# Output stores alternate between the SyncE and the GpSimd queue

## The chip, the cores and the metric

The kernel runs on one core of a Trainium2 chip. The metric is the device time of one execution in microseconds (us), the median of several runs. The profile is one further execution on the same kind of chip, recorded by the hardware profiler. Its span (first to last instruction) is a little shorter than the device time.

## The reference

A mixture-of-experts dispatch reduced to its arithmetic: each of 16 x 1024 tokens has a row of 512 floats and k = 2 weights. The output holds the row twice, each copy times one of the weights. The expert indices are an input that nothing reads.

```python
batch, seq, hidden, k = 16, 1024, 512, 2
x_expanded = x[:, :, np.newaxis, :].repeat(k, axis=2)
weights = expert_weights[..., np.newaxis]
return (x_expanded * weights).astype(np.float32)
```

So 33.6 MB of float32 are read, 67.1 MB are written, and each output element costs one multiplication.

## The kernel before, in words

The 16,384 tokens are cut into 8 groups of 2,048. In a group, each of the 128 partitions holds 16 consecutive tokens (16 "columns" of 512 floats), so that a partition's share of a load is one contiguous 32 KB row in memory. A group's load is one transfer of 4.19 MB (4,096 KB) into one of two `x_tile` buffers (`x_pool`, `bufs=2`). The group's output is two tiles of 8 columns, each 4.19 MB as well: a column holds both copies of a token. They come from a pool of four `o_tile` buffers (`o_pool`, `bufs=4`). A group thus moves three transfers of equal size: a load and two stores.

Weights: eight small loads (16 KB each, L55), one for each group, are issued on SyncE's queue at the start, ahead of all stores.

Compute: for every column, ScalarE multiplies the row by the second weight (`nc.scalar.mul`, L91) and VectorE by the first (`nc.vector.tensor_scalar`, L97). Each engine therefore runs 8 instructions for an output tile and 16 for a group, 128 in all. When both have done the eight columns of a tile, it is stored by one transfer (L105) on SyncE's queue. That store's landing is what frees the output buffer for the tile four later.

Loads: those of groups 0 and 1 are issued at the start, on ScalarE's queue (L76). The load of group i+2 takes the buffer that group i has read, so it waits for both engines' last multiply of group i. In the built program it stands on ScalarE just behind the first multiply of group i+1. That multiply in turn waits for the load of group i+1 and for a free output buffer, so the next load is issued when group i+1 starts.

The order of the work is that of the program: the framework puts a wait where a tile is read, written or reused, and gives each transfer one of a set of completion semaphores, in turn. SyncE has nothing to do but issue the weight loads and the stores. GpSimd sets four constants at the start and does nothing else. The end of the program (L134) waits for all transfers.

The lines around the change:

Of the kernel before, what the change touches and what calls it, by code (L numbers as in the profile page):

```python
# [1 line left out]

# [4 lines left out]


@with_exitstack
def kernel(  # L10
    ctx: ExitStack,
    tc: tile.TileContext,
    x: bass.AP,
    expert_indices: bass.AP,
    expert_weights: bass.AP,
    out: bass.AP,
):
    nc = tc.nc

    batch, seq, hidden = x.shape  # L20
    k = expert_weights.shape[-1]
    P = nc.NUM_PARTITIONS
    ntok = batch * seq
    assert ntok % P == 0
    A_TOTAL = ntok // P

    f32 = mybir.dt.float32
    row = k * hidden
    TX = 16
    TO = 8  # L30


    groups = [[16], [16], [16], [16], [16], [16], [16], [16]]
    assert sum(sum(g) for g in groups) == A_TOTAL

    xf = x.rearrange("b s h -> (b s) h")
    of = out.rearrange("b s k h -> (b s) (k h)")
    wf = expert_weights.rearrange("b s k -> (b s) k")

    w_pool = ctx.enter_context(tc.tile_pool(name="w_pool", bufs=1))  # L40
    x_pool = ctx.enter_context(tc.tile_pool(name="x_pool", bufs=2))
    o_pool = ctx.enter_context(tc.tile_pool(name="o_pool", bufs=4))

    w_tile = w_pool.tile([P, A_TOTAL * k], f32)

    def rows(of_all, done, T):
        return of_all[done * P : (done + T) * P, :].rearrange(
            "(p a) n -> p (a n)", a=T
        )

    weights = []
    for group in groups:
        weights.append((sum(n for _, n in weights), sum(group)))
    for at, T in weights:
        nc.sync.dma_start(out=w_tile[:, at * k : (at + T) * k], in_=rows(wf, at, T))  # L55

    tiles = []
    done = 0
    for group in groups:
        T = sum(group)  # L60
        a0 = 0
        for n in group:
            tiles.append((done, T, a0, n))
            a0 += n
        done += T

    loaded = []

    def load(i):
        if i >= len(tiles):  # L70
            return
        done, T, a0, n = tiles[i]
        x_tile = x_pool.tile([P, TX * hidden], f32)
        cols = rows(xf, done, T)[:, a0 * hidden : (a0 + n) * hidden]
        for lo, hi in [(0, P)]:
            nc.scalar.dma_start(out=x_tile[lo:hi, : n * hidden], in_=cols[lo:hi, :])  # L76
        loaded.append(x_tile)

    for i in range(2):
        load(i)  # L80
    for i, (done, T, a0, n) in enumerate(tiles):
        x_tile = loaded[i]
        outr = rows(of, done, T)
        for t in range(n):
            if t % TO == 0:
                o_tile = o_pool.tile([P, TO * row], f32)
            for kk in range(k):
                c = (done + a0 + t) * k + kk
                o = t % TO * row + kk * hidden
                if kk == 1:  # L90
                    nc.scalar.mul(  # L91
                        out=o_tile[:, o : o + hidden],
                        in_=x_tile[:, t * hidden : (t + 1) * hidden],
                        mul=w_tile[:, c : c + 1],
                    )
                    continue
                nc.vector.tensor_scalar(  # L97
                    out=o_tile[:, o : o + hidden],
                    in0=x_tile[:, t * hidden : (t + 1) * hidden],
                    scalar1=w_tile[:, c : c + 1],  # L100
                    scalar2=None,
                    op0=mybir.AluOpType.mult,
                )
            if (t + 1) % TO == 0:
                nc.sync.dma_start(  # L105
                    out=outr[:, (a0 + t + 1 - TO) * row : (a0 + t + 1) * row],
                    in_=o_tile,
                )
        load(i + 2)

# [1 line left out]
_INS = ['x', 'expert_indices', 'expert_weights']  # L112
_OUTS = [((16, 1024, 2, 512), 'float32')]


# [23 lines left out]
```

## Time and profile before

| What | Value |
|---|---|
| Time, median of 3 runs | 240.27 us (240.18 to 241.31) |
| Span of the profiled execution | 238.4 us |
| VectorE busy | 51.9 us (22%), 128 multiplies of 480 ns |
| ScalarE busy | 81.3 us (34%), 128 multiplies of 708 ns |
| HBM read, written | 33.69 MB, 67.11 MB: 423 GB/s over the span |
| A load, issue to landing | 23.2 us (median) |
| A store, issue to landing | 48.3 us (median) |

How to read the profile: ACT is ScalarE, DVE VectorE, POOL GpSimd, SP SyncE; ACTq and SPq are their instruction queues, which issue transfers. An issue is not the transfer: the issuing instruction takes some 0.33 us, while the 16 DMA engines move the data later. The rows of digits cut the span into 40 slices of about 6 us; a 9 is a slice busy for 90% or more. In the list of queues, q1 is SyncE's and q10 is ScalarE's, each with packets, MB and its packets' time as a share of 16 engines' span. In the waits, a row has the waiting engine and line, what it waited for, the sum in us, how often, and the longest. In the timeline, a row has start, length and instruction; in brackets is the idle time ahead of it with what ended it. Where a group of the timeline has several multiplies of one engine, "mean" durations include overlap of neighbours, so 8 of ScalarE's take 5.01 us and not 8 x 708 ns.

### The profile page before, as it was taken

The numbers are of one execution on the slowest core, as the hardware profiler recorded it, in microseconds if no ns is written. First come the engines' busy times: TensorE is split into PE (matmuls) and PEld (weight loads), VectorE is DVE, ScalarE is ACT, GpSimd is POOL, SyncE is SP. The second block draws the span as 40 slices with busy tenths as digits, with TensorE's granted clock in tenths as the row PEclk, the third lists the DMA queues.
The fourth block names the chain that finished last, engine by engine and source line by source line (L and its number), as shares of the span: only waits on it lengthen the run. The fifth ranks groups of instructions, "written<-read, shape, count | busy, mean of one in ns | idle before, by whom it ended". The sixth has DMA issues, their size and how long they took to land.

```text
span 238.4 us, 384 instructions
## 1 busy us (share of the span) xinstructions
DVE 51.9 (22%) x128; ACT 81.3 (34%) x129; POOL 0.2 (0%) x4
## 2 busy tenths in 40 slices
DVE  0072910055005004050230503204040235000000
ACT  0278970086207007080260803417043256200000
POOL 0000000000000000000000000000000000000000
DMA  7999999999999999999999999999999999999996
GB/s 266 441 442 357 441 429 412 423 429 429 440 440 440 437 434 434 440 440 418 423 429 423 434 440 440 434 440 434 440 429 440 434 429 412 429 429 440 440 440 264
DMA packets 4610, 100.81 MB, mean 423 GB/s; under 512 B 1536, under 2 KB 1536, under 8 KB 1536
## 3 DMA queue, kind: packets, MB, share of 16 engines
q1 hardware_dynamic: 3456, 67.24, 65.6%
q10 hardware_dynamic: 1152, 33.55, 33.2%
q14 instruction: 2, 0.02, 0.0%
HBM read 33.69 MB, written 67.11 MB: 423 GB/s over the span
## 4 chain that ended last, share of the span: by engine, by line
DMA 60%; another core or an unknown queue 12%; ACT 12%; ACTq 1%; issue 0%
DMA out_dram<-o_tile 41%; DMA x_tile<-in_x_dram 16%; ACT o_tile L91 12%; DMA w_tile<-in_expert_weights_dram 3%; ACTq L76 0%; ACTq L134 0%; ACTq L91 0%
## 5 line engine op out<-in xcount | busy, mean ns | idle before, releaser
L91 ACT ACTIVATE o_tile<-x_tile,w_tile 128x512 f32<-128x512 f32 x128 | 80.1, 708 | 113.9 <-DMA out_dram<-o_tile 96.1
L97 DVE TENSOR_SCALAR o_tile<-x_tile,w_tile 128x512 f32<-128x512 f32 x128 | 51.9, 480 | 150.4 <-DMA out_dram<-o_tile 115.6
L91 ACT ACT_TABLE_LOAD x1 | 1.3, 1283 | 8.7 <-DMA w_tile<-in_expert_weights_dram 8.7
L123 POOL MEMSET const-bfloat16-1.0<- 128x1 bf16 x1 | 0.1, 101 | 0.0
L123 POOL MEMSET const-uint8-127<- 128x1 uint8 x1 | 0.1, 101 | 0.0
L123 POOL MEMSET const-float32-0.0<- 128x1 f32 x1 | 0.1, 98 | 0.2 <-issue 0.2
L123 POOL MEMSET const-float32-1.0<- 128x1 f32 x1 | 0.1, 98 | 0.0
## 6 DMA issues: line engine op xcount, KB each, us to landing
out_dram<-o_tile SPq DMA_DIRECT2D x16, 4096.0 KB, 48.3
x_tile<-in_x_dram ACTq DMA_DIRECT2D x8, 4096.0 KB, 23.2
w_tile<-in_expert_weights_dram SPq DMA_DIRECT2D x8, 16.0 KB, 21.1
```

Of the source, the lines that this page charges most:

```text
L91: nc.scalar.mul(out=o_tile[:, o : o + hidden], in_=x_tile[:, t * hidden : (t + 1) * hidden], mul=w_tile[:, c : c + 1],)
L97: nc.vector.tensor_scalar(out=o_tile[:, o : o + hidden], in0=x_tile[:, t * hidden : (t + 1) * hidden], scalar1=w_tile[:, c : c + 1], scala ...
L123: nc = _bacc.Bacc("TRN2", target_bir_lowering=False, num_devices=1)
```

## The change

The store of a group's first output tile stays on SyncE's queue, that of its second goes to GpSimd's. Each then issues eight of the sixteen stores. Loads stay on ScalarE's queue and the weights on SyncE's. The purpose is to have the stores on two queues, so that one store need not stand behind the one before it in the same queue.

```diff
             if (t + 1) % TO == 0:
-                nc.sync.dma_start(
+
+                store = nc.sync if t // TO % 2 == 0 else nc.gpsimd
+                store.dma_start(
                     out=outr[:, (a0 + t + 1 - TO) * row : (a0 + t + 1) * row],
                     in_=o_tile,
                 )
```

`TO` is 8, and `t` runs over the group's 16 columns, so `t // TO % 2` is 0 for the first tile and 1 for the second. In the changed kernel the store's line is L107, and the end of the program is L136.

## The prediction

> **What bounds the kernel now.** I read the page's DMA rows first, since two compute engines at 22% and 34% can't be the bound.
>
> ```profile
> DVE 51.9 (22%) x128; ACT 81.3 (34%) x129; POOL 0.2 (0%) x4
> DMA  7999999999999999999999999999999999999996
> GB/s 266 441 442 357 441 429 412 423 429 429 440 440 440 437 434 434 440 440 418 423 429 423 434 440 440 434 440 434 440 429 440 434 429 412 429 429 440 440 440 264
> ...
> q1 hardware_dynamic: 3456, 67.24, 65.6%
> q10 hardware_dynamic: 1152, 33.55, 33.2%
> ```
>
> The 16 DMA engines are at 9 in every slice but the first and the last. Queue q1 (SyncE's: 16 stores of 4.19 MB and the weights) and q10 (ScalarE's: 8 loads) took 65.6 + 33.2 = 98.8% of 16 engines' span. That is 235.5 of 238.4 us, so 2.9 us are idle: by the packet records about 1.9 us before the first packet and 0.9 us after the last. Nothing is idle between. A tile of 4.19 MB at 432 GB/s is 9.7 us of all the engines; 24 of them are 233 us.
>
> Next, the waits, and the issues.
>
> ```profile
> DVE o_tile L97 <- DMA out_dram<-o_tile: 115.6, 11, 13.8
> ACT o_tile L91 <- DMA out_dram<-o_tile: 96.1, 11, 12.0
> DVE o_tile L97 <- DMA x_tile<-in_x_dram: 34.7, 3, 17.1
> ACT o_tile L91 <- DMA x_tile<-in_x_dram: 17.7, 3, 13.6
> ```
>
> ```profile
> out_dram<-o_tile SPq DMA_DIRECT2D x16, 4096.0 KB, 48.3
> x_tile<-in_x_dram ACTq DMA_DIRECT2D x8, 4096.0 KB, 23.2
> ```
>
> The compute engines wait 11 times for a store to free one of the four output buffers, and only 3 times (the first groups) for a load: output buffers hold the kernel back, and always with stores queued, 48.3 us from issue to landing, five times a tile's 9.7. A load lands 23.2 us after its issue. If one load and one store share the engines evenly it needs 2 x 9.7 = 19.4 us; the other 3.8 us pass before its first packet (the packet records say 3.9 for the load issued at 72.97). Last, the timeline, one group of 16 columns:
>
> ```profile
> 102.30 0.72 ACT L91 ACTIVATE o_tile<-x_tile,w_tile 128x512 f32<-128x512 f32 x1 [8.38 <-DMA out_dram<-o_tile]
> 102.34 3.26 DVE L97 TENSOR_SCALAR o_tile<-x_tile,w_tile 128x512 f32<-128x512 f32 x8 [10.07 <-DMA out_dram<-o_tile]
> 102.38 0.33 ACTq L76 DMA_DIRECT2D x_tile<-in_x_dram  x1
> 102.93 4.38 ACT L91 ACTIVATE o_tile<-x_tile,w_tile 128x512 f32<-128x512 f32 x7
> ...
> 131.30 0.72 ACT L91 ACTIVATE o_tile<-x_tile,w_tile 128x512 f32<-128x512 f32 x1 [8.38 <-DMA out_dram<-o_tile]
> ...
> 198.93 5.01 ACT L91 ACTIVATE o_tile<-x_tile,w_tile 128x512 f32<-128x512 f32 x8 [4.62 <-DMA out_dram<-o_tile]
> ```
>
> A group's first multiply and its load issue stand together (102.30 and 102.38), a group takes 29.0 us (131.30 - 102.30), and it moves three tiles: 3 x 9.7 = 29.1. So a load issued at a group's start lands 5.8 us (29.0 - 23.2) before the next group could use it. The last multiply ends at 203.9, 34 us before the end: stores alone fill the tail.
>
> **What the Trainium skill says.** *DMA: Bandwidth & Descriptors*, section "Issuing engines are not separate DMA queues": transfers from any engine interleave on the same 16 engines, and several issuers save only issue time. The trace agrees that there is little to save: 0.33 us per issue, hidden. Same page, "Queues, rings and completion order": each DMA engine takes the queues that have work in turn, a packet at a time. The 23.2 us above fit an even split of two. Same page, "SWDGE vs HWDGE vs iDMA": a GpSimd transfer has its descriptors written by GpSimd's cores into rings in SBUF. No run here shows it yet. *SBUF — State Buffer*, "Who interferes with whom": a two-port VectorE instruction, which a tensor_scalar can be, blocks GpSimd from the shared port, and so such a store's start. In before GpSimd issues nothing.
>
> **The change part by part.** Bytes, buffers and multiplies stay. In the built instruction order the other engines' sequences are unchanged, ScalarE still waits for a store tile by tile, and the waits on reused DMA semaphores still point to transfers long landed. Four things change.
>
> *Issue.* Eight of 16 stores leave SyncE's queue: 8 x 0.33 us less there, worth nothing, as SyncE sits waiting for the multiplies.
>
> *Descriptors.* GpSimd writes them for 8 stores. The skill's first byte is about 1 us against 0.6 (its page's "Specifications"); it is hidden wherever a few us of other transfers are queued, as they are by the reckoning below. VectorE's lock hardly matters: a store waits for ScalarE's 8 x 0.63 = 5.0 us, while VectorE's 8 take 3.26 us, and both tiles of a group (6.42 us in the opening groups) are done before ScalarE's 10. I take 0; upper end one burst, 3.3 us, once.
>
> *Row size.* Rows go as packets of 32 KB at 1,213 ns, and 128 B ones take 13 ns (packet records): about 8 ns fixed each. If software cuts rows to 4 KB, a row has 7 more, 56 ns; 1,024 rows over 16 engines make 3.6 us, at 2 KB 7.7 us. "The descriptor swizzle" (same page) has 8 KB rows whole in a 1 MiB transfer, so I take uncut: 0.
>
> *Shares.* This is the step that can move the end. With stores pending on two queues, a load gets a third and not half: 3 x 9.7 + 3.8 = 33 us from issue to landing, where the group has 29. The 5.8 us of slack are gone, so loads become the gate and stores drain in between. I reckoned this by hand from the first store at 23.6 us: a load gets 1/2 beside one busy store queue and 1/3 beside two; the next load's first packet comes 4.1 us after a landing (less when little is queued); a group's stores are issued 5.1 and 10.1 us after its start. Loads 2 to 7 (from 0) then land at about 57, 91, 124, 154, 181 and 212 us, and the store work still queued is 14.6, 10.5, 6.4, 5.7, 7.0 and 5.6 us. The queue never empties between loads: it shrinks until one store queue runs dry for a while, and the load gets its half again. So the middle costs 0. In the tail, group 7 starts at 212 and not at 189 as in before. Its first store goes out 5.1 us later and needs 1.3 us to its first packet (first issue 0.7 us, first packet 2.0). The 5.6 us of queue cover 6.4 us but for 0.8; then two tiles follow. With 0.3 for a GpSimd start that is not fully hidden the sum is +1.1 us: 240.27 + 1.1 = 241.4. The queue at the last landing is the soft number: sharing or start times a little different make it 3 to 7, so the hole is 0 to 3.4 us.
>
> **Rivals.**
> (a) *Hidden anyway.* The queue at the last landing is 6.4 us or more, as in two of the last four landings reckoned above (6.4 and 7.0). Nothing shows: 240.3. For it: transfers are saturated and bytes equal. Against: the last reckoned queue is 5.6.
> (b) *Software rows cost.* Cut at 4 KB: 240.27 + 3.6 + about 1 = 245; at 2 KB 249. For it: no such transfer in the trace. Against: 8 KB rows are whole in the skill.
> (c) *Loads starved.* If GpSimd's ring gets more than its turn (a packet of several rows), the store queue is empty at the last landing, 6.4 us idle: 247; with 1.6 us lost at each of six landings more, 256.
> (d) *Faster.* Some packets in the opening took about 2 us and not 1.2; the slice at 18 to 24 us moved 357 GB/s, not 441. Packets over 1,213 ns add 1.5 us per engine in all. If other interleaving removes them and the tail has no hole: 238.8. Against: they come at the first load and at the first store, which stay where they are. There are no other idle microseconds to win.
>
> **How the numbers follow.** Forecast (small hole in the tail) 0.45, (a) 0.30, (b) 0.11, (c) 0.08, (d) 0.06. The bound for "slower" is 241.47; over half of the forecast's spread (240.8 to 243.7) lies above it. Slower: 0.27 + 0.11 + 0.08, near 0.47; same 0.30 + 0.17 = 0.47; faster 0.06. The range goes from 239.9, leaving most of (d) out, to 246.5, which takes in the whole hole and rows cut at 4 KB, and leaves out 2 KB rows and starved loads.
>
> **What would show it.** Right: ScalarE's and VectorE's waits move from the stores to the loads (up to 8 waits each, one for each group); the median load from issue to landing rises from 23.2 to 27 to 33 us; the last multiply ends near 222 and not 203.9; DMA slices stay 9 up to the last tenth, and a dip of 1 to 3 us stands about 217. Wrong in the shares: loads still land in about 23 us and the stores remain the wait. Wrong in the row size: the GpSimd queue has more than 1,024 data packets plus increments, or a larger sum of the queues' shares x span than 235.5 us. Wrong as in (c): dips at every group.

## The result and the profile after

The changed kernel takes 253.18 us (median; 250.68 to 254.11), the kernel before 240.23 us: a ratio of 1.051 (95% interval 1.043 to 1.060). It is slower by 5%, far beyond the forecast of 241.4 us and above the range. Each profile is of one execution. The ratios here and below leave out single runs that lie more than 1.5% above the fastest of the same kernel.

The page of the changed kernel, its DMA rows and its queues (q0 is GpSimd's):

```profile
span 251.0 us, 388 instructions
...
DMA  7999999999999999999998999999999999996995
GB/s 290 435 435 355 423 407 355 397 345 418 392 402 433 402 428 428 431 402 428 418 433 355 386 428 428 428 418 350 428 465 428 433 418 423 454 392 272 433 418 251
...
q10 hardware_dynamic: 1152, 33.55, 33.2%
q1 hardware_dynamic: 2304, 33.69, 33.0%
q0 software_dynamic: 1152, 33.55, 31.0%
```

The digits hardly differ from those of before: the DMA engines still count as busy nearly everywhere. The GB/s row is what gives the change away: slices of 345 to 407 GB/s under a 9. The same bytes take longer. By the shares, packets took 98.8% of 238.4 = 235.5 us per DMA engine before and 97.2% of 251.0 = 244.0 us now. GpSimd's queue has 1,152 packets: 1,024 rows of 32 KB and 128 increments of semaphores, so its rows are not cut.

The waits, and the issues with their median time to landing:

```profile
DVE o_tile L97 <- DMA x_tile<-in_x_dram: 178.8, 8, 31.9
ACT o_tile L91 <- DMA x_tile<-in_x_dram: 144.3, 8, 28.4
```

```profile
x_tile<-in_x_dram ACTq DMA_DIRECT2D x8, 4096.0 KB, 30.3
out_dram<-o_tile SPq DMA_DIRECT2D x8, 4096.0 KB, 31.3
out_dram<-o_tile POOLq DMA_DIRECT2D x8, 4096.0 KB, 33.7
```

All waits for stores have gone; every group now waits for its load. And the timeline of the last group:

```profile
223.78 9.91 ACT L91 ACTIVATE o_tile<-x_tile,w_tile 128x512 f32<-128x512 f32 x16 [20.34 <-DMA x_tile<-in_x_dram]
```

It starts at 223.8 us, where the last one of before ended at 203.9.

**Where 12.6 us of span came from.** The packet records add up, per DMA engine (mean of 16): packets longer by 8.5 us (244.1 against 235.6, increments and weights included); idle between first and last packet 3.5 us against none; 0.6 us more from the last packet to the end of the span. The sum is 12.6. In both kernels the median packet of 32 KB takes 1,213 ns. After the first 26 us, 2 of 2,777 such packets were over that by more than 0.1 us before, and 288 of 2,775 in the changed kernel, these with a mean of 1.67 us. Of the 288, 274 are on the two hardware queues: what packets took beyond 1,213 ns after the opening sums, per DMA engine, to 4.2 us on SyncE's queue, 4.0 on ScalarE's, and 0.2 on GpSimd's own.

The long packets are not spread over the whole run. All but one of the 288 start before 174 us. From 174 to 230 us none of 700 is long, though all three queues have packets there (256 on GpSimd's, 272 on SyncE's, 172 on ScalarE's).

**The DMA engines fall out of step.** Each of these transfers raised its semaphore 16 times, once for each DMA engine, and landed with the last. The trace keeps all 16 times (us, sorted; it does not name the engines):

```text
before, a load    182.3 182.4 182.5 182.5 182.5 182.5 182.6 182.6 182.9 183.0 183.0 183.2 183.5 183.6 183.7 183.8
changed, a store   86.2  86.4  86.5  86.6  86.6  86.7  86.8  87.0  87.1  87.3  90.2  90.4  90.7  92.5  93.0  94.2
changed, load 7   212.6 212.6 212.7 212.7 212.7 212.7 212.7 212.8 214.2 214.3 216.1 217.8 217.9 218.0 223.7 223.7
```

Load 7 is that of the last group. Before, first and last are never more than 2.2 us apart; in the changed kernel up to 16.3. For the last group's load, ten DMA engines were done by 214.3, two needed until 223.7, and the group, which starts at 223.8, waited for those two.

### The profile page after: what moved, and what is told of

The parts are those of the page before. It is cut to its first block, busy times and chain, and to the rows that moved or that the text cites. A ratio compares the mean times of both kernels' runs of the same rounds, so it can differ in the third digit from the quotient of the medians.

```text
span 251.0 us, 388 instructions
## 1 busy us (share of the span) xinstructions
DVE 51.4 (20%) x128; ACT 80.7 (32%) x129; POOL 4.6 (2%) x12
## 3 DMA queue, kind: packets, MB, share of 16 engines
q10 hardware_dynamic: 1152, 33.55, 33.2%
q0 software_dynamic: 1152, 33.55, 31.0%
## 4 chain that ended last, share of the span: by engine, by line
DMA 88%; DVE 2%; issue 2%; POOLq 0%; ACT 0%; DVEq 0%; ACTq 0%
DMA x_tile<-in_x_dram 85%; DMA w_tile<-in_expert_weights_dram 3%; DVE o_tile L97 2%; POOLq L136 0%; ACT o_tile L91 0%; DVEq L136 0%; ACTq L91 0%; DVEq L97 0%; POOLq L107 0%
## 5 line engine op out<-in xcount | busy, mean ns | idle before, releaser
L91 ACT ACTIVATE o_tile<-x_tile,w_tile 128x512 f32<-128x512 f32 x128 | 79.4, 708 | 144.4 <-DMA x_tile<-in_x_dram 144.3
L97 DVE TENSOR_SCALAR o_tile<-x_tile,w_tile 128x512 f32<-128x512 f32 x128 | 51.4, 480 | 178.8 <-DMA x_tile<-in_x_dram 178.8
L107 POOL DMA_DIRECT2D out_dram<-o_tile x8 | 4.4, 550 | 229.7 <-ACT o_tile L91 229.7
## 6 DMA issues: line engine op xcount, KB each, us to landing
x_tile<-in_x_dram ACTq DMA_DIRECT2D x8, 4096.0 KB, 30.3
out_dram<-o_tile SPq DMA_DIRECT2D x8, 4096.0 KB, 31.3
out_dram<-o_tile POOLq DMA_DIRECT2D x8, 4096.0 KB, 33.7
```

Of the source, the lines that this page charges most:

```text
L91: nc.scalar.mul(out=o_tile[:, o : o + hidden], in_=x_tile[:, t * hidden : (t + 1) * hidden], mul=w_tile[:, c : c + 1],)
L97: nc.vector.tensor_scalar(out=o_tile[:, o : o + hidden], in0=x_tile[:, t * hidden : (t + 1) * hidden], scalar1=w_tile[:, c : c + 1], scala ...
L107: store.dma_start(out=outr[:, (a0 + t + 1 - TO) * row : (a0 + t + 1) * row], in_=o_tile,)
```

## The experiments

Three theories. A: the third busy queue (two of stores and one of loads) is at fault, through the load's share or through the rotation itself. B: a GpSimd queue harms its neighbours. C: two queues that write neighbouring 32 KB rows harm each other. Diffs are against the changed kernel.

| Run | Busy queues | Time, us (range) | Ratio to before, 95% | Packets, us too long | Landings apart, median / max |
|---|---|---|---|---|---|
| before | 2 | 240.2 | 1 | 1.6 | 0.9 / 2.2 |
| changed | 3 | 253.2 | 1.043 to 1.060 | 10.0 | 6.0 / 16.3 |
| all stores on GpSimd | 2 | 242.0 | 1.003 to 1.008 | 2.1 | 1.3 / 3.1 |
| stores on ScalarE and SyncE | 2 | 242.8 | 1.006 to 1.016 | 3.3 | 0.9 / 4.3 |
| alternating by group | 3 | 249.6 | 1.028 to 1.041 | 5.3 | 4.8 / 18.8 |
| second tile's rows far away | 3 | 254.8 | 1.049 to 1.061 | 10.9 | 4.9 / 16.7 |
| three x, three output buffers | 3 | 250.1 | 1.033 to 1.042 | 4.1 | 3.7 / 13.8 |
| the same, one store queue | 2 | 240.8 | 1.000 to 1.003 | 1.5 | 1.4 / 2.5 |
| 16 KB store rows | 3 | 243.3 | 1.007 to 1.014 | 1.8 | 2.3 / 5.8 |
| the same, one store queue | 2 | 247.3 | 1.017 to 1.030 | 3.9 | 4.6 / 12.0 |

"Too long" sums, per DMA engine, what packets took beyond 1,213 ns (611 ns for 16 KB), the opening included. "Apart" is between a transfer's first and last engine, in us, over all loads and stores. The packet and landing columns are of one execution each.

**1. All stores on GpSimd**

```diff
-                store = nc.sync if t // TO % 2 == 0 else nc.gpsimd
+                store = nc.gpsimd
```

> All sixteen stores on GpSimd, loads on ScalarE: two busy queues, one of them software. Theory A (a third busy queue takes the load's share and lengthens packets): about 240 us, loads land in about 23 us and the waits are for stores, packets beyond 1,213 ns add under 2 us per DMA engine. Theory B (a GpSimd queue by itself lengthens the packets of the other queues): 248 us or more, long packets among ScalarE's loads.

241.99 us (241.63 to 242.75). The waits are those of before:

```profile
DVE o_tile L97 <- DMA out_dram<-o_tile: 105.8, 10, 15.0
ACT o_tile L91 <- DMA out_dram<-o_tile: 96.5, 11, 13.2
```

Packets are 2.1 us too long in all, against 1.6. Theory B falls as it was put: GpSimd as the only store queue costs 0.55%, not 5%.

**2. Loads on GpSimd, stores on ScalarE and SyncE**

```diff
-            nc.scalar.dma_start(out=x_tile[lo:hi, : n * hidden], in_=cols[lo:hi, :])
+            nc.gpsimd.dma_start(out=x_tile[lo:hi, : n * hidden], in_=cols[lo:hi, :])
-                store = nc.sync if t // TO % 2 == 0 else nc.gpsimd
+                store = nc.scalar if t // TO % 2 == 0 else nc.sync
```

> Three queues with the roles changed: loads on GpSimd, stores alternate between ScalarE (first tile) and SyncE (second). Theory A: as in the changed kernel, 248 to 255 us, loads land in about 30 us or more, waits for loads, a hole of about 4 us before the last group's stores. Theory B with GpSimd's part in the transfers equal (8 of 24): long packets on the hardware queues as well, same time. Theory C (two store queues that write neighbouring 32 KB rows are what lengthens packets): also slow. This run says only whether GpSimd must carry stores.

Four times: 244.01, 281.61, 285.9 and 286.31 us. None is in theory A's 248 to 255, and no ratio and no cause is drawn from so wide a scatter. The profile is of the 286.31 and tells of that execution alone: landings of one transfer up to 41 us apart, and whole slices in which most DMA engines are idle while a few finish:

```profile
DMA  7999999999999999999899994698972996039940
```

Packets too long come to 9.8 us per DMA engine and idle time to 37.7. So DMA engines can fall far apart with no store on GpSimd's queue.

**3. Alternating by group**

```diff
-                store = nc.sync if t // TO % 2 == 0 else nc.gpsimd
+                store = nc.sync if i % 2 == 0 else nc.gpsimd
```

> Stores alternate by group and not by tile: both tiles of an even group on SyncE, both of an odd one on GpSimd. Three queues as in the changed kernel, but the tiles that write neighbouring 32 KB rows follow one another in one queue. Theory A: still slow, 245 to 254 us. Theory C (neighbouring rows written at the same time): long packets go, leaving the load's gate and the hole in the tail, 240.3 + 4 = about 244 us.

249.56 us (247.82 to 251.97): in A's band, well above C's 244. Packets too long fall to 5.3 us in the one execution profiled, so the order of the stores may matter for the size of the loss, but landings are up to 18.8 us apart.

**4. Two hardware queues**

```diff
-                store = nc.sync if t // TO % 2 == 0 else nc.gpsimd
+                store = nc.scalar if t // TO % 2 == 0 else nc.sync
```

> No GpSimd: the first tile's store on ScalarE's queue, which also carries the loads, the second tile's on SyncE's. Two hardware queues, two store streams. Theory A: no long packets, about 240 us if the load's place behind a store in its own queue does not let the queues run dry. Theory C: long packets, over 244 us. Theory B: no long packets.

242.79 us (242.39 to 244.12).

```profile
DVE o_tile L97 <- DMA x_tile<-in_x_dram: 164.9, 8, 28.7
ACT o_tile L91 <- DMA x_tile<-in_x_dram: 122.0, 8, 25.2
```

Every group waits for its load here too, because loads stand behind stores in ScalarE's queue. That is nearly the wait of the changed kernel (178.8 and 144.3), and the time is 1.1% over before. So loads as the gate (the thing that each group waits for) cost little by themselves.

**5 and 6. Store rows of 16 KB, with two store queues and with one**

```diff
-    TO = 8
+    TO = 4
-    o_pool = ctx.enter_context(tc.tile_pool(name="o_pool", bufs=4))
+    o_pool = ctx.enter_context(tc.tile_pool(name="o_pool", bufs=8))
```

> The changed kernel with output tiles of 4 columns and 8 buffers (same memory): store rows of 16 KB beside load rows of 32 KB, so that a load that gets every third turn gets half of the bytes. Shares theory (the load's third is what makes it the gate, and dry queues and the hole follow): loads land in about 24 us again, the waits go back to the stores, no hole in the tail, 241 to 243 us with 1 us for the extra packets. Three-queue theory (any rotation of three queues lengthens packets and takes the DMA engines out of step, whatever the shares): 248 us or more, 16 engines' landings of one transfer 5 us or more apart.

243.29 us (242.09 to 244.28); loads land in 23.6 us, the waits are for stores, packets are 1.8 us too long. That is close to what the shares theory said (241 to 243 us), and far from the three-queue theory's 248. The control, with `store = nc.sync` as well:

> The control to the run with rows of 16 KB: output tiles of 4 columns, 8 buffers, all stores on SyncE. Two queues: no long packets beyond the first loads and stores, landings of one transfer within 3 us, 240.3 + 1 = about 241 us by both theories.

247.32 us (244.99 to 249.19): both theories missed. With two queues whose rows are 32 and 16 KB, packets are 3.9 us too long. The last store's landings are 238.6 to 239.2 us for eleven DMA engines and 240.2, 243.2, 243.3, 244.3 and 244.5 for the others. Falling out of step does not need three queues.

**7 and 8. Three x buffers and three output buffers, with two store queues and with one**

```diff
-    x_pool = ctx.enter_context(tc.tile_pool(name="x_pool", bufs=2))
-    o_pool = ctx.enter_context(tc.tile_pool(name="o_pool", bufs=4))
+    x_pool = ctx.enter_context(tc.tile_pool(name="x_pool", bufs=3))
+    o_pool = ctx.enter_context(tc.tile_pool(name="o_pool", bufs=3))
-    for i in range(2):
+    for i in range(3):
-        load(i + 2)
+        load(i + 3)
```

> The changed kernel with three x buffers and three output buffers, and loads issued three groups ahead: a load may take a group longer before anyone waits for it. Shares theory: loads are no gate, the hole is gone, 240 to 243 us. Three-queue theory: long packets and engines out of step stay while all three queues have work, about 245 to 249 us. With three output buffers, at most three stores are queued, which could add up to a few us in either.

250.05 us (249.55 to 256.9). Its only two waits for loads are in the opening:

```profile
DVE o_tile L97 <- DMA out_dram<-o_tile: 156.3, 11, 36.6
ACT o_tile L91 <- DMA out_dram<-o_tile: 118.3, 11, 21.6
DVE o_tile L97 <- DMA x_tile<-in_x_dram: 16.7, 2, 13.3
```

Packets are 4.1 us too long, the DMA engines idle 6.7 us, and the last store lands on thirteen DMA engines by 241.9 and on three at 246.4 to 246.9. The control:

> The control to the run with three x and three output buffers (250 us): the same buffers, all stores on SyncE. If the two store queues cost in that run, this one takes 240 to 243 us with long packets under 2 us per DMA engine and a transfer's 16 landings within 3 us. If its loss came from having only three output buffers, this one takes 248 us or more as well.

240.79 us (240.03 to 242.2), packets 1.5 us too long, landings within 2.5. With equal buffers, and with no group after the opening waiting for a load, the second store queue costs 9.3 us. The spans differ by 9.5 us: 2.6 by longer packets, 6.3 by idle DMA engines, 0.6 at the end. The gate is thus not the cause: the shares theory falls as the explanation of the 12 us.

**9. The last two groups on SyncE**

```diff
-                store = nc.sync if t // TO % 2 == 0 else nc.gpsimd
+                store = nc.sync if t // TO % 2 == 0 or i >= 6 else nc.gpsimd
```

> The changed kernel, but all four stores of the last two groups on SyncE: the last load shares with one store queue at most. If the hole before the last group's stores costs 3.9 us, and comes from the last load's late landing, this run is 3 to 4 us shorter than the changed kernel, 248 to 250 us, with the long packets of the first six groups still there. If all of the loss follows from the gate, it does not tell more; if the hole is not from the last load's share, no gain.

252.3 us (251.95 to 254.4): no gain that can be measured. In the changed kernel, the group-6 store on GpSimd's queue landed at 225.9 us on the first DMA engine and at 229.8 on the last, and the next group's packets began at 229.7. So most engines had a hole of nearly 4 us, and the last two had none. The hole in the changed kernel, by stretches (start and end, length, busy time of VectorE, ScalarE and GpSimd, clock, the DMA engines' busy share, GB/s):

```profile
190.00:226.00 36.00, 8.61 (x22) 12.13 (x20) 0.53 (x1) 1.00 0.99 426
226.00:230.00 4.00, 4.00 (x11) 4.00 (x8) 0.00 (x0) 1.00 0.42 180
```

Here the hole is gone, and the last store lands at 245.0 to 248.9 us, again 4 us apart. In the changed kernel, which had the hole, the last store's landings are 0.2 us apart. The hole was time in which the others waited for the slowest; without it, the same wait stands at the end.

**10. Rows of the second tile written far away**

```diff
+                far = rows(of, (done + 64) % A_TOTAL, T)
+                dst = outr if t // TO % 2 == 0 else far
                 store.dma_start(
-                    out=outr[:, (a0 + t + 1 - TO) * row : (a0 + t + 1) * row],
+                    out=dst[:, (a0 + t + 1 - TO) * row : (a0 + t + 1) * row],
```

> The changed kernel, but the second tile of each group is written to the place of the group four further on (modulo 8), so that the output has those rows in another place; bytes, row size and queues are as in the changed kernel. Neighbour theory (two queues that write neighbouring 32 KB rows lengthen each other's packets): the long packets go, 10 us to about 4 us per DMA engine, and the time falls to 244 to 247 us. Rotation theory (it is the third queue in the rotation, not the addresses): no change, 250 to 254 us, packets after a load and a GpSimd store are long as often as before.

254.75 us (252.55 to 256.42), 10.9 us of long packets. Theory C falls.

**11. Loads in 16 KB rows**

```diff
-        for lo, hi in [(0, P)]:
-            nc.scalar.dma_start(out=x_tile[lo:hi, : n * hidden], in_=cols[lo:hi, :])
+        for lo, hi in [(0, n * hidden // 2), (n * hidden // 2, n * hidden)]:
+            nc.scalar.dma_start(out=x_tile[:, lo:hi], in_=cols[:, lo:hi])
```

> The changed kernel with each load cut into two of 16 KB rows beside store rows of 32 KB: beside two store queues, a load now gets one fifth of the bytes and not one third. Shares theory: loads are a worse gate, a group's load takes up to 45 us until store queues run dry, more idle time, 255 us or more. If shares do not matter, the time stays at 250 to 254 us.

254.41 us (251.78 to 257.69), ratio 1.046 to 1.061: not told apart from the changed kernel. A smaller share for the loads did not cost more, another miss of the shares theory.

**12 to 15. All rows of 16 KB**

```diff
-    TX = 16
-    TO = 8
+    TX = 8
+    TO = 4
-    groups = [[16], [16], [16], [16], [16], [16], [16], [16]]
+    groups = [[8, 8]] * 8
-    x_pool = ctx.enter_context(tc.tile_pool(name="x_pool", bufs=2))
-    o_pool = ctx.enter_context(tc.tile_pool(name="o_pool", bufs=4))
+    x_pool = ctx.enter_context(tc.tile_pool(name="x_pool", bufs=4))
+    o_pool = ctx.enter_context(tc.tile_pool(name="o_pool", bufs=8))
-    for i in range(2):
+    for i in range(4):
-        load(i + 2)
+        load(i + 4)
```

> The changed kernel with all rows halved: loads in halves of 8 columns with four x buffers, output tiles of 4 columns with eight buffers, three queues. A load again has one third of the bytes. Shares theory: loads are the gate again, long packets and engines out of step return, 247 us or more. Row-size theory (it was the 16 KB rows that helped in the run with half-size output tiles): about 243 us, loads wait-free.

Four times: 242.04, 247.2, 249.52 and 252.22 us. The profile, of the 242.04, had three queues, all 16 halves waiting for their loads, and yet packets only 1.6 us too long and landings within 1.2 us. Neither theory had named that: loads were waited for at 242 us. One program gave both cases; two further runs of it tell them apart.

> The kernel with all rows halved once more, one look. Its four times were 242.0, 247.2, 249.5 and 252.2 us, and the profile was that of the 242.0. Step theory (what costs is that the 16 DMA engines fall out of step; third queue and gate are nearly free while they stay in step): a run of 246 us or more shows the 16 landings of one transfer 5 us or more apart, and packets well over 611 ns; a run of 242 us shows neither. If a slow run has its landings together and its packets short, the step theory falls.

> The same kernel a further time, one look, for the same purpose: time and spread of landings go together, or the step theory falls.

241.95 us and 249.5 us; the kernel before took 240.0 to 241.9 in between on that chip. The DMA row of the 241.95, then of the 249.5:

```profile
DMA  7999999999999999999999999999999999999995
```

```profile
span 247.7 us, 456 instructions
...
DMA  6999999999999999999999999999999999999930
GB/s 268 410 375 423 431 431 434 423 431 429 429 430 429 430 429 429 431 426 431 423 439 426 429 429 426 434 431 429 431 426 431 429 437 429 431 426 434 434 169 19
```

Nothing is wrong until the last two slices: 169 and 19 GB/s. The last store's landings say why:

```text
241.95 us run   237.5 to 238.7 (16 engines)
249.5 us run    237.7 to 238.8 (14 engines), 241.1, 246.3
```

Two of 16 DMA engines were late, by 2.3 and 7.5 us, and 7.5 us is what the run lost (span 247.7 against 240.2). The distance had grown step by step, from 1.8 us at 47 to 8.6 at 215. It fits single packets of about 0.87 us in place of 0.61: 42 of 5,562 after the opening, against 2 of 5,568 in the other run. Together they are 11.0 us over, and the two late engines are 9.8 us late. The expectation held for the landings (over 5 us; median 5.2, up to 8.7) and missed for the packets, of which few were long. Gate and third queue are the same in both runs, so neither sets their difference. In size this is another case than the changed kernel: there packets were longer by 8.5 us on the average DMA engine, here by 0.35. The control, `store = nc.sync`:

> The control with all rows halved and all stores on SyncE, two queues. Step theory: landings of a transfer stay within 3 us, and the time is 240.3 us and about 1 us for the additional packets, with little scatter between runs. If halved rows alone make the runs scatter, this one scatters from 242 to 252 us too.

244.33 us (243.66 to 244.57), packets 2.8 us too long, landings up to 6.9 us apart: more than the expected 241 us and 3 us, with less scatter than with three queues. One store queue is no better here than two in step.

## Why the prediction was wrong, point by point

- *What bounds the kernel*: right. The DMA engines bound it before and after, and no run here is faster than before.
- *Issue, descriptors, row size*: right. GpSimd's queue carried uncut rows at 1,213 ns; all sixteen stores there cost 0.55%. Rival (b) is out. Its second sign, a larger sum of shares x span than 235.5 us, did come (244.0), but from longer packets and not from cut rows.
- *Shares*: the direction was right. Waits moved to the loads, 8 for each engine, and the median load took 30.3 us, within the 27 to 33 named. The reckoning had loads 2 to 7 land at 57, 91, 124, 154, 181 and 212 us. Their first DMA engine had them at 59, 95, 125, 150, 181 and 213 us, and their last at 62, 99, 134, 165, 194 and 224. So it was about right for the fastest engine, perhaps in part by luck, since it left out the longer packets; it was 5 to 13 us short for the slowest, for which the group waits. (The packet times in it stand some 0.2 us late on the profile's clock: the first packet is at 1.7 us, not 2.0. No step turns on that.)
- *"So the middle costs 0"*: this step failed. I priced every packet at 1,213 ns, whatever the number of queues in turn, and treated 16 DMA engines as one. Packets took 8.5 us more per engine, unevenly, and each landing waited for the slowest, so that engines also stood idle for 3.5 us. In the forecast's sum (+1.1 us) the first term was 0; it is the larger part of 12.6.
- *The tail*: the dip came at 226 to 230 us, where about 217 was named, and for most DMA engines it was a little longer than the upper end of my hole (3.4). The last multiply ended at 233.7 us and not near 222. But run 9 shows that taking it away wins nothing measurable: it was waiting for the slowest engines.
- *Rival (c)* had a time of 247 to 256, but by GpSimd's ring getting more than its turn. The store medians (33.7 us on GpSimd's queue, 31.3 on SyncE's) show nothing of that. The right time there would have been for a wrong reason.
- *The skill.* "DMA: Bandwidth & Descriptors", section "Issuing engines are not separate DMA queues", says that several issuers save only issue time. For the gain this held. But I drew from it that there is no loss either, which it does not say, and this case measures 5%.

**What stays open.** Shown: the loss goes with longer packets and with single DMA engines falling behind; neither the load gate, nor GpSimd's queue as the only store queue, nor neighbouring rows causes it; at 32 KB rows the second store queue does (the change itself, and runs 7 and 8). Not shown: what lengthens a packet. A third queue in the rotation is not enough by itself: in the changed kernel no packet was long from 174 to 230 us, and with 16 KB rows in step 2 of 5,568 were. Nor are three queues needed: run 6 had long packets with two. In every run with three busy queues one of them is GpSimd's, so it is not shown whether a third hardware queue would cost the same. The trace does not say whether the late DMA engines are always the same ones. Nor is it shown why one run of the same program stays in step and another does not.

## What to carry to other kernels

Where the DMA engines are already busy in every slice, as here, don't count on another queue for bandwidth, and price in a loss: here 5%, though only about 1% with 16 KB store rows (run 5). Read the GB/s row and not only the busy digits, and compare the queues' shares times the span before and after: more busy time for the same bytes means longer packets. A transfer lands with the slowest of 16 engines, so a reckoning that treats them as one is a lower bound: here it was 5 to 13 us short.

## What was not expected of the hardware

- A 32 KB packet is not always 1,213 ns: with three queues 288 of 2,775 took 1.67 us in the mean, all but one of them before 174 us.
- One program, run repeatedly, took 242.0 to 252.2 us (all rows 16 KB), another 244.0 to 286.3 (loads on GpSimd), while the kernel before stayed within 239.9 to 242.3.
- Two queues with rows of 32 and 16 KB cost 2.4% against 32 KB on both (run 6; interval 1.7 to 3.0%).
